# Seven block products for half the k-tiles of the output groups, on a TensorE-bound decoder trunk

## The chip, the cores and the metric

The kernel runs on one core of a Trainium2 chip. Its time is the device time of one execution in microseconds (us), less being better. Five engines work side by side, each with its own in-order queue: TensorE (PE, with PEld for the loads of its stationary operand), VectorE (DVE), ScalarE (ACT), GpSimd (POOL) and SyncE (SP). SP and POOL issue the DMAs spoken of here. They meet through semaphores alone.

## The reference

A decoder trunk of two layers, one of gated linear attention (GLA, 4 heads) and one of retention (8 heads), on 256 tokens of width 2048, all in float32. Cut to what matters:

```python
h = x
h = h + gla_mixer(rms_norm(h, gla_norm[0]), gla_w_in[0], ...)        # ends with (o * silu(gate)) @ w_out
h = h + retention_mixer(rms_norm(h, ret_norm[0]), ..., ret_w_in[0])  # ends with (o * silu(gate)) @ w_out
return rms_norm(h, final_norm)
```

`w_in` has 10240 columns (GLA) and 12288 (retention), `w_out` is 4096 x 2048 in both. Nearly all of the work is the product of 256 tokens with these weights, each read once from HBM.

## The kernel before, in words

The weights are laid out as 60 groups of 2048 rows and 512 columns. A group is 16 k-tiles of 128 rows, read in four chunks of 1 MB (`raw`, four k-tiles) by SP. For precision every chunk is split in two, `hi` (rounded to TensorE's fp32r format, ScalarE, line 152) and `lo` (the rest, VectorE, line 153), two k-tiles at a time: such a piece, 128 x 1024, is called a unit here. The pools hold three raw chunks, three `hi` and three `lo` tiles; a tile is written again only when its last reader is done, and `emit_split` runs two units ahead of the matmuls.

The tokens are split in the same way and kept on chip, as `xhl` (layer input) and `ogt` (mixer output, transposed, 16 k-tiles for one half of the inner width). A product of a k-tile with a group takes three matmuls per token half of 128 tokens: hi x hi, hi x lo, lo x hi (`mm3`, lines 189 to 191). `group_x` does this for the 16 k-tiles and both token halves, into two PSUM banks: 96 matmuls of 512 columns.

Heads come first (`gla_head`, `ret_head`): one group for q and k, then groups for v and the gate, with the scores' work of small tiles fitted in by a queue of generators (`side`; `advance` takes one step after each unit, `drain_side` takes all). After half of the heads of a layer `out_half` multiplies `ogt` with the four groups of that half of `w_out`, and `out_cols` (line 678) adds each result to `resid` on VectorE. That happens four times, under the names ga, gb (GLA) and ra, rb (retention), 16 groups in all. In gb the sums are also transposed back into `xhl` (`transpose_out`) for the next layer; in rb the last group is done by `out_tail`, which also norms and stores.

The order on each engine is set by a scheduler from the program's dependences; queues are in order when the kernel runs. POOL issues the few small loads (`dm`, `gg`, `gb`, `pos`, `fn`) and does some additions of the GLA scores.

Of the kernel before, what the change touches and what calls it, by code (L numbers as in the profile page):

```python
# [10 lines left out]
F32 = mybir.dt.float32  # L11
F32R = mybir.dt.float32r
BF16 = mybir.dt.bfloat16
I32 = mybir.dt.int32
AF = mybir.ActivationFunctionType
ALU = mybir.AluOpType

P = 128
SEQ = 256
# [3 lines left out]
GW = 512  # L23
SUB = 2
NSUB = NKT // SUB
CHUNK = 4
# [29 lines left out]
def kernel(  # L56
# [17 lines left out]
    nc = tc.nc  # L74
    pool = lambda name, bufs, **kw: ctx.enter_context(tc.tile_pool(name=name, bufs=bufs, **kw))
    one = pool("one", 1)
    raw_p = pool("raw", 3)
    hi_p = pool("hi", 3)
    lo_p = pool("lo", 3)
    v_p = pool("v", 2)  # L80
# [20 lines left out]
    per_raw = CHUNK // SUB  # L101
    raws_per_group = NKT // CHUNK

    last0 = (n_groups - 1) * NSUB

    def emit_raw(parts=1):
        c = emitted["raw"]
        if c >= n_groups * raws_per_group:
            return
        t = raw_p.tile([P, CHUNK, GW], F32, tag="raw", name=f"raw{c}")  # L110
        g, j = divmod(c, raws_per_group)
        src = w_all[g, :, j * CHUNK * GW : (j + 1) * CHUNK * GW].rearrange("p (k n) -> p k n", n=GW)
        step = CHUNK // parts
        raws[c] = t
        emitted["raw"] += 1

        def load(k, n=1):
            sl = slice(k * step, (k + n) * step)
            nc.sync.dma_start(t[:, sl, :], src[:, sl, :])

        if parts > 1:
            return load
        load(0)
# [15 lines left out]

    def emit_split(pieces=1, between=None):  # L140
        i = emitted["sub"]
        if i >= n_groups * NSUB:
            return
        c, j = divmod(i, per_raw)
        while emitted["raw"] <= min(c + DMA_LOOK, n_groups * raws_per_group - 1):
            emit_raw()
        src = raws[c][:, j * SUB : (j + 1) * SUB, :]
        hi, lo = split_tiles(i)
        step = SUB // pieces
        for k in range(pieces):  # L150
            sl = slice(k * step, (k + 1) * step)
            a = nc.scalar.activation(hi[:, sl], src[:, sl], AF.Copy)  # L152
            b = nc.vector.tensor_tensor(lo[:, sl], src[:, sl], hi[:, sl].bitcast(F32), ALU.subtract)  # L153
            if i == 0:
                first(a, b)
                if k == 0:
                    between()
        splits[i] = (hi, lo)
        if j == per_raw - 1:
            del raws[c]  # L160
        emitted["sub"] += 1

# [3 lines left out]
    def advance(n=1):  # L166
        for _ in range(n):
            while side:
                try:
                    next(side[0])  # L170
                    break
                except StopIteration:
                    side.popleft()

    def drain_side():
        while side:
            advance()

    def next_weights():
        i = state["sub"]  # L180
        while emitted["sub"] <= min(i + LOOK, n_groups * NSUB - 1):
            emit_split()
        state["sub"] += 1
        return splits.pop(i)
# [8 lines left out]
    def group_x(lhs, name, hook=None, deadline=None, bank=None):  # L193
        bank = bank or (acc_p, "acc")
        ps = [bank[0].tile([P, GW], F32, tag=bank[1], name=f"{name}_ps{t}") for t in range(2)]
        for j in range(NSUB):
            if j == deadline:
                drain_side()
            hi, lo = next_weights()
            for q in range(SUB):  # L200
                for t in range(2):
                    mm3(ps[t], lhs, j * SUB + q, t, hi, lo, q)
            if hook is not None:
                hook(j)
            advance()
        return ps

    def group_w(rhs, name, extra=None):
        ps = [acc_p.tile([P, 2, SEQ], F32, tag="acc", name=f"{name}_ps{c}") for c in range(4)]
# [383 lines left out]
    def gla_head(h):  # L593
        hw = {}
        if h > 1:
            side.appendleft(gla_decay(h, hw))
        ps = group_w(xhl, f"gqk{h}", first_group if h == 0 else None)
        drain_side()

        def scores():  # L600
            yield from gla_scores(h, hw)

        qk = t4_p.tile([P, 4, SEQ], F32, tag="qk", name=f"qk{h}", bufs=1)
        evac_w(ps, qk, f"gqk{h}")
        hw["qk"] = qk
        if h == 0:
            side.append(gate_low_rank())
        if h < 2:
            side.append(gla_decay(h, hw))
        if h > 0:  # L610
            side.append(scores())
        r, r2 = rr[:, 0, :], rr[:, 1, :]
        os_, sgs, vs = [], [], []
        sso = st_p.tile([P, 2, 2], F32, tag="sso", name=f"sso{h}")

        def o_part(gi):
            g = 2 * h + gi
            if gi == 0:
                drain_side()
            po = o_mms(hw["sc"], vs[gi], f"go{g}")  # L620
            o = o_p.tile([P, 2, GW], F32, tag="o", name=f"go{g}")
            for t in range(2):
                nc.scalar.activation(o[:, t, :], po[t], AF.Copy, scale=r[:, t : t + 1])
                nc.scalar.activation(po[t], o[:, t, :], AF.Square, accum_out=sso[:, t, gi : gi + 1])
            os_.append(o)
            if gi == 1:
                side.append(og_part(0))

        def og_part(gj):
            g = 2 * h + gj  # L630
            if gj == 0:
                yield
                m = st_p.tile([P, 2], F32, tag="m", name=f"hm{h}")
                hr = st_p.tile([P, 2], F32, tag="hr", name=f"hr{h}")
                nc.vector.tensor_tensor(m, sso[:, :, 0], sso[:, :, 1], ALU.add)
                nc.vector.tensor_scalar(m, m, 1.0 / 1024.0, EPS, ALU.mult, ALU.add)
                rsqrt(hr, m, 2, f"hr{h}")
                hw["hr"] = hr
                yield
            o, sg, hr = os_[gj], sgs[gj], hw["hr"]  # L640
            for t in range(2):
                nc.vector.scalar_tensor_tensor(
                    o[:, t, :], o[:, t, :], hr[:, t : t + 1], sg[:, t, :], ALU.mult, ALU.mult
                )
            yield
            yield from transpose_out(
                lambda t, j: o[:, t, j * P : (j + 1) * P],
                (g % 4) * 4,
                S_HG + 4 * g,
                ogt,  # L650
                f"got{g}",
            )

        for gi in range(2):
            g = 2 * h + gi

            def v_hook(j):
                if h > 0 and gi == 1 and j == 1:
                    o_part(0)

            def g_hook(j):
                if h == 0 and gi == 1 and j == 5:
                    o_part(0)
                if gi == 1 and j == (6 if h == 0 else 2):
                    o_part(1)

            if h == 0 and gi == 1:
                drain_side()
                side.append(scores())
            pv = group_x(xhl, f"gv{g}", v_hook)  # L670
            vs.append(v_evac(pv, r2, f"gv{g}"))
            sgs.append(g_evac(group_x(xhl, f"gg{g}", g_hook), r, f"gsg{g}"))
        drain_side()
        side.append(og_part(1))

    def out_cols(c, ps, t, first, final):
        dst = resid[:, t, c * GW : (c + 1) * GW]
        nc.vector.tensor_tensor(dst, ps, dst, ALU.add)
        if not first:
            square_sum(t, c)  # L680
        if final:
            nc.vector.tensor_tensor(dst, dst, fns[c], ALU.mult)

    fns = {}

    def out_half(first, final, name):
        for c in range(4):
            if final:
                fns[c] = gn_p.tile([P, GW], F32, tag="gn", name=f"fn{c}")
                nc.gpsimd.dma_start(fns[c], final_norm[c * GW : (c + 1) * GW].partition_broadcast(P))  # L690
                if c == 3:
                    break
            ps = group_x(ogt, f"{name}{c}", deadline=5)
            for t in range(2):
                out_cols(c, ps[t], t, first, final)
            if first or final:
                continue
            for _ in transpose_out(
                lambda t, j: resid[:, t, c * GW + j * P : c * GW + (j + 1) * P],
                4 * c,  # L700
                S_RN + 4 * c,
                xhl,
                f"xt2_{c}",
            ):
                pass

    def rsqrt_col(y, m, name):
        s = st_p.tile([P, 4], F32, tag="nw", name=f"{name}_nw")
# [128 lines left out]
    def ret_head(h):  # L837
# [17 lines left out]
        def o_part(j):  # L855
# [19 lines left out]
            for t in range(2):  # L875
                nc.vector.scalar_tensor_tensor(
                    o[:, t, :], o[:, t, :], a[:, t : t + 1], gb, ALU.mult, ALU.add
                )
            hw["o"] = o

        sg = g_evac(group_x(xhl, f"rg{h}", o_part), r, f"rsg{h}")

# [9 lines left out]

    for h in range(2):
        gla_head(h)
    side.append(rotary_tables())
    out_half(True, False, "ga")
    for h in range(2, 4):
        gla_head(h)
    out_half(False, False, "gb")
# [110 lines left out]
```

## Time and profile before

| what | value |
|---|---|
| three runs | 1417.96, 1420.44, 1420.67 us, median 1420.44 |
| profiled execution, first to last instruction | 1418.0 us |
| PE, DVE, ACT, POOL busy | 99%, 64%, 49%, 3% |
| loads by SP: 1 MB chunks, issue to landing | 238, median 4.8 us |
| the four output stages in the trace | 255 to 344, 582 to 673, 953 to 1041, 1320 to 1410 us |

In the rows below, a group of instructions is told as: line, engine, operation, output <- inputs, shapes, count | busy us, mean ns of one | idle us of the engine just before them and what ended most of it. PEclk gives the granted TensorE clock in tenths in 40 slices of the span. A row by stretches starts with the stretch, its length, then busy us (and instructions) of PE, PEld, DVE, ACT, POOL, the clock, the DMA engines' busy share and GB/s. In a DMA row stand queue, count, KB each and median us from issue to landing. A timeline row begins with start and length in us.

### The profile page before, as it was taken

The page shows a single profiled execution, that of the slowest core. Times are in us where ns is not written, and L with a number is a line of the kernel's source. Part 1 is how long each engine was busy: PE and PEld are TensorE (multiplying, and loading weights), DVE is VectorE, ACT ScalarE, POOL GpSimd, SP SyncE. Part 2 cuts the span into 40 slices and gives each one's busy share as a digit, 9 for nine tenths or more (in the row PEclk, how much of TensorE's full clock was granted, in tenths as well). Part 3 has the DMA queues.
Part 4 walks back from the last instruction along what each step waited for, and adds up shares of the span by engine and source line. Part 5 has one row for each costly group of instructions (what it writes and reads, how often), then busy time and mean ns, then how long its engine had stood idle before and what let it go on. Part 6 is the DMA issues. An engine that isn't in the chain of part 4 may idle for free.

```text
span 1418.0 us, 17505 instructions
## 1 busy us (share of the span) xinstructions
PE 1403.7 (99%) x6800; PEld 1181.0 (83%) x6800; DVE 907.0 (64%) x1423; ACT 693.1 (49%) x896; POOL 46.5 (3%) x99
## 2 busy tenths in 40 slices
PE   8999999999999999999999999999999999999997
PEld 6888888888888888888888888888888888888887
DVE  6685796645855774655666666665547666666664
ACT  4575655534554645554544444444344444444453
POOL 1001020000010020000000000000000000000000
PEclk9999999999999999999999999999999999999999
DMA  8654555555555555455555555555555555555562
GB/s 286 238 179 148 186 183 178 178 194 188 181 178 178 173 199 183 169 187 179 184 196 191 194 193 195 185 198 179 200 186 184 196 183 198 183 204 175 209 215 90
DMA packets 40147, 266.72 MB, mean 188 GB/s; under 512 B 4848, under 2 KB 5360, under 8 KB 9344
## 3 DMA queue, kind: packets, MB, share of 16 engines
q1 hardware_dynamic: 36816, 257.05, 52.1%
q0 software_dynamic: 2240, 7.21, 1.6%
q10 hardware_dynamic: 1008, 1.35, 0.3%
q8 instruction: 53, 0.87, 0.2%
q14 instruction: 30, 0.25, 0.0%
HBM read 263.49 MB, written 2.10 MB: 187 GB/s over the span
## 4 chain that ended last, share of the span: by engine, by line
PE 98%; DVE 0%; ACT 0%; DMA 0%; issue 0%; ACTq 0%
PE rqk_ps L232 8%; PE gv_ps L189 4%; PE gg_ps L189 4%; PE rv_ps L189 4%; PE gv_ps L190 4%; PE rv_ps L190 4%; PE gg_ps L190 4%; PE gv_ps L191 4%; PE gg_ps L191 4%; PE rv_ps L191 4%; PE rg_ps L189 4%; PE rg_ps L190 4%; PE rg_ps L191 4%; PE rqk_ps L233 4%; PE gqk_ps L232 4%; PE gb_ps L189 2%
## 5 line engine op out<-in xcount | busy, mean ns | idle before, releaser
L153 DVE TENSOR_TENSOR lo<-raw,hi 128x1024 fp32r<-128x1024 f32 (+1 forms) x473 | 576.6, 1222 | 425.0 <-ACT hi L152 424.4
L152 ACT ACTIVATE hi<-raw 128x1024 fp32r<-128x1024 f32 (+1 forms) x473 | 499.5, 1057 | 608.3 <-PE rg_ps L191 104.6
L232 PE MATMUL rqk_ps<-xhl,hi 128*128 128x512 f32 x480 | 166.9, 398 | 0.0
L233 PE MATMUL rqk_ps<-xhl,lo 128*128 128x256 f32 x480 | 126.4, 280 | 0.0
L232 PEld LDWEIGHTS rqk_ps<-xhl,hi 128*128 128x128 f32 x480 | 88.8, 188 | 17.5
L190 PE MATMUL rv_ps<-lo,xhl 128*128 128x512 f32 x256 | 100.4, 392 | 0.0
L190 PE MATMUL gv_ps<-lo,xhl 128*128 128x512 f32 x256 | 100.4, 392 | 0.0
L190 PE MATMUL gg_ps<-lo,xhl 128*128 128x512 f32 x256 | 100.4, 392 | 0.0
L191 PE MATMUL gv_ps<-hi,xhl 128*128 128x512 f32 x256 | 100.2, 392 | 0.0
L191 PE MATMUL gg_ps<-hi,xhl 128*128 128x512 f32 x256 | 100.0, 391 | 0.0
L191 PE MATMUL rv_ps<-hi,xhl 128*128 128x512 f32 x256 | 99.7, 389 | 0.0
L190 PE MATMUL rg_ps<-lo,xhl 128*128 128x512 f32 x256 | 99.6, 389 | 0.0
L191 PE MATMUL rg_ps<-hi,xhl 128*128 128x512 f32 x256 | 99.6, 389 | 0.0
L189 PE MATMUL gv_ps<-hi,xhl 128*128 128x512 f32 x256 | 93.2, 391 | 0.0
L189 PE MATMUL rv_ps<-hi,xhl 128*128 128x512 f32 x256 | 92.1, 390 | 0.0
L233 PEld LDWEIGHTS rqk_ps<-xhl,lo 128*128 128x128 f32 x480 | 89.1, 189 | 3.4
L189 PE MATMUL rg_ps<-hi,xhl 128*128 128x512 f32 x256 | 91.8, 389 | 0.0
L189 PE MATMUL gg_ps<-hi,xhl 128*128 128x512 f32 x256 | 91.7, 391 | 0.0
L232 PE MATMUL gqk_ps<-xhl,hi 128*128 128x512 f32 x216 | 73.3, 397 | 0.0
L191 PEld LDWEIGHTS rv_ps<-hi,xhl 128*128 128x128 f32 x256 | 48.1, 188 | 10.0
L191 PEld LDWEIGHTS rg_ps<-hi,xhl 128*128 128x128 f32 x256 | 48.1, 188 | 10.0
L190 PEld LDWEIGHTS rg_ps<-lo,xhl 128*128 128x128 f32 x256 | 48.1, 188 | 10.0
(273 smaller groups left out, 2405.3 us busy)
## 6 DMA issues: line engine op xcount, KB each, us to landing
raw<-in_w_all SPq DMA_DIRECT2D x238, 1024.0 KB, 4.8
resid<-in_x_n SPq DMA_DIRECT2D x2, 1024.0 KB, 8.5
gg<-in_gn_g POOLq DMA_DIRECT2D x8, 256.0 KB, 3.8
gb<-in_gn_b POOLq DMA_DIRECT2D x8, 256.0 KB, 4.5
raw<-in_w_all SPq DMA_DIRECT2D x3, 512.0 KB, 6.4
xt<-in_x_t SPq DMA_DIRECT2D x3, 512.0 KB, 8.0
dm<-in_dmat POOLq DMA_DIRECT2D x8, 192.0 KB, 2.6
fn<-in_final_norm POOLq DMA_DIRECT2D x4, 256.0 KB, 4.2
```

What stands on the lines that cost most here:

```text
L152: a = nc.scalar.activation(hi[:, sl], src[:, sl], AF.Copy)
L153: b = nc.vector.tensor_tensor(lo[:, sl], src[:, sl], hi[:, sl].bitcast(F32), ALU.subtract)
L189: mm(ps, xh, hi[:, q, :], start=kt == 0, stop=False)
L190: mm(ps, xh, lo[:, q, :], start=False, stop=False)
L191: mm(ps, xl, hi[:, q, :], start=False, stop=kt == NKT - 1)
L232: mm(ps[c], wh, rhs[:, kt, :, :], start=kt == 0, stop=False)
L233: mm(ps[c][:, 0, :], wl, rhs[:, kt, 0, :], start=False, stop=False)
```

## The change

Output groups are taken in pairs p and q (same rows of `w_out`, two neighbouring column groups), except the last two of rb, which stay as they were: seven pairs. For k-tiles 0 to 7 the 2 x 2 blocks (two token halves, two halves of those k-tiles, two column groups) are multiplied by a scheme of seven block products in place of eight; k-tiles 8 to 15 are multiplied as before (`both`). The new function `pair_x` does a pair:

- A block product (`seven`) is four k-tiles with one set of 128 tokens: 12 matmuls, from two units.
- Its token operands are plain halves or four sums of halves, which `token_combos` makes once per output half on VectorE and ScalarE, in the `side` queue of the last head.
- Its weight operands are chunk sums that are made in the raw tile: after x (first p chunk) is split, a DMA from POOL with `accum_op=ALU.add` adds another chunk to it in place, then again, three times in all; y (second q chunk) gets one. So x is split four times, y twice, and a pair has 22 units where two groups had 16. `plan_pair` writes the order.
- One PSUM bank, `a`, carries three products after each other without being cleared: after the first, second and third product `join` adds it to or subtracts it from `resid` on VectorE; it then takes k-tiles 8 to 15 of its own block. A second bank `b` is joined twice.
- The raw pool has four tiles instead of three (x stays for a whole pair), and the space for POOL's DMA descriptors is halved to 8192.

```diff
-    raw_p = pool("raw", 3)
+    raw_p = pool("raw", 4)
...
+    def plan_pair(gp, gq):
+        x = plan_chunk(gp, 0)
+        plan_units(x, False, [(x, gq, 0)])
+        plan_units(plan_chunk(gp, 1))
+        v0 = plan_chunk(gp, 2)
+        plan_units(v0)
+        y = plan_chunk(gq, 1)
+        plan_units(x, False, [(x, gq, 1)])
+        plan_units(y, False, [(y, gq, 0)])
+        v1 = plan_chunk(gp, 3)
+        units.append((v1, 0, False, ()))
+        plan_units(x, False, [(x, gp, 1)])
+        units.append((v1, 1, True, ()))
+        plan_units(y)
+        plan_units(x)
+        for j in (2, 3):
+            plan_units(plan_chunk(gq, j))
...
         splits[i] = (hi, lo)
-        if j == per_raw - 1:
+        for x, g, k in then:
+            nc.gpsimd.dma_start(raws[x], chunk_src(g, k), accum_op=ALU.add)
+        if last:
             del raws[c]
...
+        seven(a, plain(0, 0), True, True)
+        join(0, 0, a, ALU.add)
+        seven(c11, plain(1, 0), True, False)
+        c21 = acc_p.tile([P, GW], F32, tag="acc", name=f"{name}_ps21")
+        both((c11, c21), 0, (False, True), (False, False))
+        both((c11, c21), 1, (False, False), (False, False))
+        while cname not in combos:
+            advance()
+        b = lev_p.tile([P, GW], F32, tag="lev", name=f"{name}_psb")
+        seven(b, mixed(0), True, True)
+        join(0, 1, b, ALU.subtract)
+        join(1, 1, b, ALU.add)
+        c12 = acc_p.tile([P, GW], F32, tag="acc", name=f"{name}_ps12")
+        seven(c12, mixed(2), True, False)
+        drain_side()
+        both((c11, c21), 2, (False, False), (False, False))
+        seven(a, mixed(1), False, True)
+        join(0, 1, a, ALU.subtract)
+        both((c11, c21), 3, (False, False), (True, False))
+        seven(a, mixed(3), False, True)
+        join(1, 0, a, ALU.subtract)
+        done(0, 0, c11)
+        seven(c21, plain(1, 1), False, True)
+        done(1, 0, c21)
+        for j in range(4):
+            both((c12, a), j, (False, False), (j == 3, j == 3))
+        done(0, 1, c12)
+        done(1, 1, a)
...
+            def join(t, n, ps, op):
+                c = 2 * pair + n
+                dst = resid[:, t, c * GW : (c + 1) * GW]
+                with tc.high_priority():
+                    nc.vector.tensor_tensor(dst, dst, ps, op)
...
-    nc = bacc.Bacc("TRN2", target_bir_lowering=False, num_devices=1)
+    nc = bacc.Bacc("TRN2", target_bir_lowering=False, num_devices=1, dynamic_dma_scratch_size=8192)
```

The token sums, in the same diff:

```diff
+    def token_combos(lhs, name):
+        full = []
+        for half in range(2):
+            f = t4_p.tile([P, CHUNK, SEQ], F32, tag="t4", name=f"{name}_f{half}")
+            src = lhs[:, half * CHUNK : (half + 1) * CHUNK]
+            nc.vector.tensor_tensor(f, src[:, :, 0].bitcast(F32), src[:, :, 1].bitcast(F32), ALU.add)
...
+                nc.vector.tensor_tensor(u, a21, a22, ALU.subtract)
+                nc.vector.scalar_tensor_tensor(s, u, -1.0, a11, ALU.mult, ALU.subtract)
...
+                nc.vector.tensor_tensor(c[:, 0], a12, s, ALU.add)
+                nc.vector.tensor_tensor(c[:, 1], a11, a21, ALU.add)
...
+            nc.scalar.activation(d[:, 0], c, AF.Copy)
+            nc.vector.tensor_tensor(d[:, 1], c, d[:, 0].bitcast(F32), ALU.subtract)
```

More of the change, by code (lines that the diff above doesn't have):

```diff
@@ L102, with plan_chunk, plan_units, plan_group @@
     raws_per_group = NKT // CHUNK
-    last0 = (n_groups - 1) * NSUB
+    chunks, units = [], []
+    def plan_chunk(g, j):
+        chunks.append((g, j))
+        return len(chunks) - 1
+    def plan_units(c, last=True, then=()):
+        for half in range(per_raw):
+            end = half == per_raw - 1
+            units.append((c, half, last and end, then if end else ()))
+    def plan_group(g):
+        for j in range(raws_per_group):
+            plan_units(plan_chunk(g, j))
+    def plan_pair(gp, gq):
[15 more added lines that the diff above has]
+            plan_units(plan_chunk(gq, j))
+    def plan_all():
+        g = 0
+        for stage, heads in (("gla", 2), ("gla", 2), ("ret", 4), ("ret", 4)):
+            for _ in range(heads * (5 if stage == "gla" else 3)):
+                plan_group(g)
+                g += 1
+            plan_pair(g, g + 1)
+            if g + 4 == n_groups:
+                plan_group(g + 2)
+                plan_group(g + 3)
+            else:
+                plan_pair(g + 2, g + 3)
+            g += 4
+    plan_all()
+    last0 = len(units) - NSUB
+    def chunk_src(g, j):
+        return w_all[g, :, j * CHUNK * GW : (j + 1) * CHUNK * GW].rearrange("p (k n) -> p k n", n=GW)
     def emit_raw(parts=1):
         c = emitted["raw"]
-        if c >= n_groups * raws_per_group:
+        if c >= len(chunks):
             return
         t = raw_p.tile([P, CHUNK, GW], F32, tag="raw", name=f"raw{c}")
-        g, j = divmod(c, raws_per_group)
-        src = w_all[g, :, j * CHUNK * GW : (j + 1) * CHUNK * GW].rearrange("p (k n) -> p k n", n=GW)
+        src = chunk_src(*chunks[c])
         step = CHUNK // parts
@@ L141, in emit_split @@
         i = emitted["sub"]
-        if i >= n_groups * NSUB:
+        if i >= len(units):
             return
-        c, j = divmod(i, per_raw)
-        while emitted["raw"] <= min(c + DMA_LOOK, n_groups * raws_per_group - 1):
+        c, j, last, then = units[i]
+        while emitted["raw"] <= min(c + DMA_LOOK, len(chunks) - 1):
             emit_raw()
@@ L180, in next_weights @@
         i = state["sub"]
-        while emitted["sub"] <= min(i + LOOK, n_groups * NSUB - 1):
+        while emitted["sub"] <= min(i + LOOK, len(units) - 1):
             emit_split()
@@ L206, in group_x, with product @@
         return ps
+    def product(ps, a, hi, lo, q, start, stop):
+        xh, xl = a
+        mm(ps, xh, hi[:, q, :], start=start, stop=False, skip_group_check=True)
+        mm(ps, xh, lo[:, q, :], start=False, stop=False, skip_group_check=True)
+        mm(ps, xl, hi[:, q, :], start=False, stop=stop, skip_group_check=True)
+    def token_combos(lhs, name):
[4 more added lines that the diff above has]
+            nc.vector.tensor_tensor(f, src[:, :, 0].bitcast(F32), src[:, :, 1].bitcast(F32), ALU.add)
+            full.append(f)
+            yield
+        a11, a21 = full[0][:, :, 0:P], full[0][:, :, P:SEQ]
+        a12, a22 = full[1][:, :, 0:P], full[1][:, :, P:SEQ]
+        got = []
+        u, s = None, None
+        for half in range(2):
+            c = t4_p.tile([P, 2, CHUNK, P], F32, tag="t4", name=f"{name}_c{half}")
+            if half == 0:
+                u, s = c[:, 0], c[:, 1]
+                nc.vector.tensor_tensor(u, a21, a22, ALU.subtract)
+                nc.vector.scalar_tensor_tensor(s, u, -1.0, a11, ALU.mult, ALU.subtract)
+            else:
+                nc.vector.tensor_tensor(c[:, 0], a12, s, ALU.add)
+                nc.vector.tensor_tensor(c[:, 1], a11, a21, ALU.add)
+            yield
+            d = v_p.tile([P, 2, 2, CHUNK, P], F32R, tag="v", name=f"{name}_d{half}")
+            nc.scalar.activation(d[:, 0], c, AF.Copy)
+            nc.vector.tensor_tensor(d[:, 1], c, d[:, 0].bitcast(F32), ALU.subtract)
+            got.append(d)
+            yield
+        combos[name] = tuple((got[i][:, 0, k], got[i][:, 1, k]) for i, k in ((0, 0), (0, 1), (1, 0), (1, 1)))
@@ new lines, with pair_x, seven, plain @@
+    combos = {}
+    def pair_x(lhs, name, cname, join, done):
+        a = lev_p.tile([P, GW], F32, tag="lev", name=f"{name}_psa")
+        c11 = acc_p.tile([P, GW], F32, tag="acc", name=f"{name}_ps11")
+        def seven(ps, get, start, stop):
+            for half in range(2):
+                hi, lo = next_weights()
+                for q in range(SUB):
+                    k = half * SUB + q
+                    product(ps, get(k), hi, lo, q, start and k == 0, stop and k == CHUNK - 1)
+            advance()
+        def plain(part, t):
+            return lambda k: tuple(lhs[:, part * CHUNK + k, i, t * P : (t + 1) * P] for i in range(2))
+        def mixed(n):
+            return lambda k: tuple(x[:, k] for x in combos[cname][n])
+        def both(ps, j, start, stop):
+            hi, lo = next_weights()
+            for q in range(SUB):
+                for t in range(2):
+                    kt = 2 * CHUNK + j * SUB + q
+                    x = tuple(lhs[:, kt, i, t * P : (t + 1) * P] for i in range(2))
+                    product(ps[t], x, hi, lo, q, start[t] and q == 0, stop[t] and q == SUB - 1)
+            advance()
+        seven(a, plain(0, 0), True, True)
[5 more added lines that the diff above has]
+        while cname not in combos:
+            advance()
+        b = lev_p.tile([P, GW], F32, tag="lev", name=f"{name}_psb")
[18 more added lines that the diff above has]
+        done(1, 1, a)
@@ L627, in o_part @@
                 side.append(og_part(0))
+                if h % 2:
+                    side.append(token_combos(ogt, "gb" if h == 3 else "ga"))
         def og_part(gj):
@@ L684, with out_half, finish @@
     fns = {}
[L686 to L697, printed above, removed]
+    def out_half(first, final, name, later=None):
+        def finish(t, c, ps):
+            out_cols(c, ps, t, first, final)
+            if first or final or t == 0:
+                return
             for _ in transpose_out(
@@ L705, in out_half, with load_fn @@
                 pass
+        for pair in range(1 if final else 2):
+            if pair == 1 and later is not None:
+                side.append(later)
+            for c in (2 * pair, 2 * pair + 1) if final else ():
+                load_fn(c)
+            def join(t, n, ps, op):
[3 more added lines that the diff above has]
+                    nc.vector.tensor_tensor(dst, dst, ps, op)
+            pair_x(ogt, f"{name}{pair}", name, join, lambda t, n, ps: finish(t, 2 * pair + n, ps))
+        if final:
+            load_fn(2)
+            load_fn(3)
+            ps = group_x(ogt, f"{name}2", deadline=5)
+            for t in range(2):
+                out_cols(2, ps[t], t, first, final)
+    def load_fn(c):
+        fns[c] = gn_p.tile([P, GW], F32, tag="gn", name=f"fn{c}")
+        nc.gpsimd.dma_start(fns[c], final_norm[c * GW : (c + 1) * GW].partition_broadcast(P))
     def rsqrt_col(y, m, name):
@@ L879, in o_part @@
             hw["o"] = o
+            if h % 4 == 3:
+                side.append(token_combos(ogt, "rb" if h == 7 else "ra"))
         sg = g_evac(group_x(xhl, f"rg{h}", o_part), r, f"rsg{h}")
@@ L894 @@
         gla_head(h)
-    side.append(rotary_tables())
-    out_half(True, False, "ga")
+    out_half(True, False, "ga", rotary_tables())
     for h in range(2, 4):
```

## The prediction

> **What bounds the kernel now.** I read the page's busy shares and its chain first, then the largest groups.
>
> ```profile
> PE 1403.7 (99%) x6800; PEld 1181.0 (83%) x6800; DVE 907.0 (64%) x1423; ACT 693.1 (49%) x896; POOL 46.5 (3%) x99
> ...
> PEclk9999999999999999999999999999999999999999
> DMA  8654555555555555455555555555555555555562
> ...
> PE 98%; DVE 0%; ACT 0%; DMA 0%; issue 0%; ACTq 0%
> ...
> L153 DVE TENSOR_TENSOR lo<-raw,hi 128x1024 fp32r<-128x1024 f32 (+1 forms) x473 | 576.6, 1222 | 425.0 <-ACT hi L152 424.4
> L152 ACT ACTIVATE hi<-raw 128x1024 fp32r<-128x1024 f32 (+1 forms) x473 | 499.5, 1057 | 608.3 <-PE rg_ps L191 104.6 <-PE rqk_ps L232 78.0 <-PE gg_ps L191 72.9
> ```
>
> TensorE is the chain (98%), at full clock. The two split engines wait on each other and on TensorE; the DMA engines are a little over half used. So fewer matmuls is a real gain, as long as hi and lo still arrive in time. How much room they have shows in the timeline of one plain output group.
>
> ```profile
> 967.69 0.62 PE L189 MATMUL ra_ps<-hi,ogt 128*128 128x512 f32 x2
> ...
> 967.95 1.06 ACT L152 ACTIVATE hi<-raw 128x1024 fp32r<-128x1024 f32 x1 [1.67 <-PE ra_ps L191]
> ...
> 969.04 1.23 DVE L153 TENSOR_TENSOR lo<-raw,hi 128x1024 fp32r<-128x1024 f32 x1 [1.50 <-ACT hi L152]
> ...
> 970.41 0.62 PE L189 MATMUL ra_ps<-hi,ogt 128*128 128x512 f32 x2
> 970.61 1.06 ACT L152 ACTIVATE hi<-raw 128x1024 fp32r<-128x1024 f32 x1 [1.60 <-PE ra_ps L191]
> ...
> 973.13 0.62 PE L189 MATMUL ra_ps<-hi,ogt 128*128 128x512 f32 x2
> ```
>
> A unit (two k-tiles, 12 matmuls) takes 970.41 to 973.13, 2.72 us, so one matmul has 0.2267 us (the 389 ns of the groups overlap). A split starts 0.2 us after TensorE leaves the unit three back (970.41 to 970.61: the buffers are three deep), takes 1.06 + 1.23 us and leaves VectorE idle 1.5 us per unit.
>
> **The matmuls.** In a block product (a unit of the new `seven`) a unit feeds one token half only, as the order on TensorE shows at the second ga pair. Before:
>
> ```order
> L189 MATMUL ga1_ps0_2424<-hi89_2406,ogt_101 128x512
> L190 MATMUL ga1_ps0_2424<-lo89_2407,ogt_101 128x512
> L191 MATMUL ga1_ps0_2424<-hi89_2406,ogt_101 128x512
> L189 MATMUL ga1_ps1_2425<-hi89_2406,ogt_101 128x512
> L190 MATMUL ga1_ps1_2425<-lo89_2407,ogt_101 128x512
> L191 MATMUL ga1_ps1_2425<-hi89_2406,ogt_101 128x512
> ```
>
> After (psa is the chained bank):
>
> ```order
> L262 MATMUL ga1_psa_2568<-hi103_2549,ogt_101 128x512
> L263 MATMUL ga1_psa_2568<-lo103_2550,ogt_101 128x512
> L264 MATMUL ga1_psa_2568<-hi103_2549,ogt_101 128x512
> L262 MATMUL ga1_ps11_2569<-hi104_2572,ogt_101 128x512
> L263 MATMUL ga1_ps11_2569<-lo104_2573,ogt_101 128x512
> ```
>
> A k-tile's weights now serve 3 matmuls instead of 6. Per pair, 8 block products of 12 matmuls become 7: 12 fewer, in 7 pairs 84 x 0.2267 = **-19.0 us**. The price is units: 22 per pair instead of 16 (42 more splits in all), 14 of them only 6 x 0.2267 = 1.36 us long.
>
> **Joins among short units.** VectorE needs 1.23 of those 1.36 us for lo, and now also five joins per pair (0.68 us each):
>
> ```profile
> L678 DVE TENSOR_TENSOR resid<-ra_ps,resid 128x512 f32<-128x512 f32 x8 | 5.1, 682 | 0.0
> ```
>
> On VectorE in the second ga pair, before (one group's end, then the next):
>
> ```order
> L678 TENSOR_TENSOR resid_99<-ga0_ps0_2231,resid_99 128x512
> L678 TENSOR_TENSOR resid_99<-ga0_ps1_2232,resid_99 128x512
> L153 TENSOR_TENSOR lo90_2429<-raw45_2326,hi90_2428 128x1024
> L153 TENSOR_TENSOR lo91_2445<-raw45_2326,hi91_2444 128x1024
> L153 TENSOR_TENSOR lo92_2463<-raw46_2388,hi92_2462 128x1024
> ```
>
> After (raw47 is x, raw50 is y, raw51 a plain chunk; lo112 is unit 10 of the pair, counted from 0):
>
> ```order
> L203 TENSOR_TENSOR lo111_2681<-raw50_2570,hi111_2680 128x1024
> L859 TENSOR_TENSOR resid_99<-resid_99,ga1_psb_2667 128x512 x2
> L203 TENSOR_TENSOR lo112_2701<-raw51_2598,hi112_2700 128x1024
> L203 TENSOR_TENSOR lo113_2711<-raw47_2474,hi113_2710 128x1024
> L203 TENSOR_TENSOR lo114_2732<-raw47_2474,hi114_2731 128x1024
> L203 TENSOR_TENSOR lo115_2749<-raw51_2598,hi115_2748 128x1024
> L203 TENSOR_TENSOR lo116_2759<-raw50_2570,hi116_2758 128x1024
> L859 TENSOR_TENSOR resid_99<-resid_99,ga1_psa_2568 128x512
> ```
>
> Two joins stand ahead of lo112, with three short units behind it. In a run of short units lo arrives 0.4 us ahead of need (two units, 2.72, plus the 0.23 of the first hi matmul, less 0.2 + 1.06 + 1.23 + 0.06); two joins are 1.36, VectorE's own gaps hold 0.3, so unit 10 is late by 0.7, the unit behind the first join by 0.1 to 0.2. I take 0.8 per pair, **+6 us**; ends 0 and all joins, 5 x 0.68 x 7 = 24. The chained bank itself is cheap: a join is done within about 2 us of its product, and a 2.72 us unit lies between the products of the chain.
>
> **The adding DMAs.** On POOL, before, at head 1's scores and after them head 2's:
>
> ```order
> L586 TENSOR_TENSOR s32_1_1535<-s32_1_1535,m1_1788 128x2x32 x2
> L586 TENSOR_TENSOR s32_1_1535<-s32_1_1535,m1_1788 128x64 x2
> L586 TENSOR_TENSOR s32_2_3067<-s32_2_3067,m2_3320 128x64 x2
> L586 TENSOR_TENSOR s32_2_3067<-s32_2_3067,m2_3320 128x32x2 x2
> L586 TENSOR_TENSOR s32_2_3067<-s32_2_3067,m2_3320 128x16x4 x2
> ```
>
> After:
>
> ```order
> L928 DMA pos_2593<-in_positions 128x256
> L210 DMA raw40_2074<-in_w_all 128x2048 x2
> L210 DMA raw43_2250<-in_w_all 128x2048
> L210 DMA raw40_2074<-in_w_all 128x2048
> L210 DMA raw47_2474<-in_w_all 128x2048 x2
> L210 DMA raw50_2570<-in_w_all 128x2048
> ```
>
> Four 1 MB adds per pair, 28 in all, stand between the two heads' work, each held until the splits of its chunk are read; behind them on POOL only work of the next head waits (in the last pair a row of final_norm). ScalarE, in order, waits for each add, and all later splits with it. With TensorE's unit 0 at time 0, the units give each add a budget:
>
> - x, first add: split of unit 1 ends at -0.2; unit 6 is due at 4 x 1.36 + 2 x 2.72 = 10.9, its split 2.2 earlier (1.06 + 1.23 + hand-over - 0.23). Budget 8.9 us.
> - x, second: the split of unit 7 starts when unit 4 is done (8.4), ends at 10.9 with the handovers; unit 11 is due at 10.9 + 4 x 1.36 + 2.72 + 0.8 = 19.9. Budget 19.9 - 2.2 - 10.9 = 6.8, say 6.7 with semaphores.
> - y: split of unit 9 ends at 14.9, unit 14 is due at 25.3: 8.2.
> - x, third: split of unit 12 ends at 20.1, unit 16 is due at 28.0: 5.7; and 4.7 once the second add has been the wait.
>
> So with L us from issue to landing a pair loses nothing up to L = 5.7, then L - 5.7, and above 6.7 (L - 6.7) + (L - 4.7) = 2L - 11.4.
>
> What is L? The trace has no add. Nearest:
>
> ```profile
> raw<-in_w_all SPq DMA_DIRECT2D x238, 1024.0 KB, 4.8
> gg<-in_gn_g POOLq DMA_DIRECT2D x8, 256.0 KB, 3.8
> gb<-in_gn_b POOLq DMA_DIRECT2D x8, 256.0 KB, 4.5
> dm<-in_dmat POOLq DMA_DIRECT2D x8, 192.0 KB, 2.6
> ...
> GB/s 415 360 0 0 0 186 295 404 426 87 11 0 164 197 426 404 229 0 0 153 131 382 470 262 0 0 44 164 328 437 382 44 0 0 186 251 426 426 109 0
> ```
>
> The same bytes by SP's queue land in 4.8 (low end, if reading the target costs nothing and POOL's queue starts as soon). The last row (1000 to 1030 us, slices of 0.75) shows 426 GB/s while a load streams: 1.05 MB in 2.46 us. If source and target are read one after the other, L is 4.8 + 2.46 = 7.3; and POOL's 256 KB take 3.8 to 4.5, up to 1.8 more than their bytes' share of 4.8 explains (4.8 - 0.75 x 2.46 = 3.0): high end 9.1. I take 7.0, near the doubled read, with some overlap of the two: 2.6 per pair, **+18 us**; ends 0 and 6.8 x 7 = 48.
>
> The Trainium skill ("Collectives: The Full Stack", section on the bandwidth ceiling) holds that an adding DMA is slow not for the add but for its two source reads through one ring, about half a copy's rate. By it L would be 7.3 and the sum some 4 us higher; no run here shows it yet.
>
> DMA load: 7 loads and 4 adds per pair, 11 to 15 MB of reads where 8 were, at 0.55 share now: 0.76 to 1.0. That alone is no bound, at the upper end nearly one.
>
> **Other work that loses its cover.**
>
> ```profile
> L258 DVE SCALAR_TENSOR_TENSOR ogt<-got_tp,smalls,ogt 128x256 fp32r<-128x256 f32 x32 | 14.3, 477 | 0.9 <-ACT ogt L257 0.6
> L642 DVE SCALAR_TENSOR_TENSOR go<-go,hr,gsg 128x512 f32<-128x512 f32 x16 | 11.5, 747 | 0.4
> L808 DVE TENSOR_TENSOR ra<-rqk,trig 128x1024 f32<-128x1024 f32 x8 | 9.8, 1224 | 0.3
> L811 DVE TENSOR_TENSOR rb<-rqk,trig 128x512 f32<-128x512 f32 x8 | 5.5, 685 | 0.0
> ...
> 230.00:255.00 25.00, 25.00 (x116) 20.80 (x115) 15.75 (x28) 13.53 (x20) 0.00 (x0) 1.00 0.49 168
> ...
> 931.00:953.00 22.00, 22.00 (x99) 18.22 (x98) 16.10 (x31) 7.95 (x9) 1.07 (x2) 1.00 0.57 208
> ...
> L488 ACT ACT_TABLE_LOAD x4 | 5.1, 1283 | 0.1
> L487 ACT ACTIVATE ya<-y,smalls 128x256 f32<-128x256 f32 x8 | 3.8, 478 | 0.0
> ```
>
> The last head's output still passes through VectorE in the first pair of ga and gb: between the lo of units 1 and 2, 4 x 0.477 + 2 x 0.747 = 3.4 us where 1.5 are free, so 2 late each; the transposes of the next layer's input in gb's second pair I put at 2. ScalarE's decay work of head 2 (4 x 0.478 + 1.28 = 3.2 us) stands ahead of a short-unit stretch's hi in ga's first pair, where x's second add is awaited anyway: 0, or 2 if that add is early. **+6** (ends 0 and 14). The token sums cost VectorE 4 x 1.22 + 4 x 0.69 = 7.7 us per half, four times, in the last gate group. In the GLA window it has 25 - 15.75 = 9.3 idle (fits), in the retention window 22 - 16.1 = 5.9: 1.8 over, twice, **+3**. ScalarE's 2.1 fit in both windows.
>
> **Sum.** -19.0 + 6 + 18 + 6 + 3 = +14. The profiled execution is itself 1418.0 us, 2.4 under the median of 1420.44; on the median: **1434 us**, slower by 1.0%.
>
> **Rivals.**
> - *The add costs a load* (L to 5.7). The GB/s row speaks for it: the engines idle half the time. The adds vanish: -4, 1416 us; if the side work hides too, 1406. It decides from L = 5.9 down. Chance 0.33 of a gain beyond 0.2%.
> - *It cancels* (L about 6.2: 0.5 x 7 = 4, against the -4 above): 1418 to 1423, chance 0.12. A difference of 0.2% (2.8 us) is what a measurement of this kernel can tell.
> - *The queue or the add is slower still* (L over 9.1, loads of SP interleaved with it): from 1463 up, chance 0.11. Here single waits pass 3 us. The Trainium skill ("TensorE: Matmul & The Clock Gate") says that the clock halves after about 3.4 us of idleness. PEclk is 9 in every slice here, so no run yet shows it; a digit under 9 in the out stages would.
>
> The forecast itself has 0.44. Slower in all: 0.44 + 0.11 = 0.55. The range 1406 to 1463 leaves out most of the third rival and about 0.08 of the first.
>
> **What would show it.** 84 fewer matmuls at 0.227; "ACT hi <- DMA raw" rising from nothing to some 18 us or more, at the third and fourth use of x; landing of raw<-in_w_all on POOL's queue near 7 us; VectorE's lo after the psb joins late by under 1 us. A landing near 5, or waits on DMA near zero, makes the forecast wrong; if it is slower with adds near 5, the splits are the cause.

## The result and the profile after

The changed kernel takes 1457.7 us (median of 1451.4 to 1462.8) against 1420.2 us: ratio 1.027, 95% interval 1.0254 to 1.0286. It is slower by 37.5 us where I had forecast 14. The profiled execution has a span of 1456.1 us, 38.1 more than before. Busy times, clock and DMA share in slices, the chain, the two split groups, and the loads on the two queues, from the page:

```profile
PE 1404.6 (96%) x6716; PEld 1172.4 (81%) x6716; DVE 997.2 (68%) x1532; ACT 740.8 (51%) x946; POOL 75.1 (5%) x127
...
PEclk9999999999999999999999999999999999999999
DMA  8554555968554555789565555569865555555881
...
PE 24%; DMA 3%; issue 1%; DVE 1%; ACT 1%; ACTq 0%; POOLq 0%
...
L203 DVE TENSOR_TENSOR lo<-raw,hi 128x1024 fp32r<-128x1024 f32 (+1 forms) x515 | 623.9, 1220 | 368.3 <-ACT hi L202 367.1
L202 ACT ACTIVATE hi<-raw 128x1024 fp32r<-128x1024 f32 (+1 forms) x515 | 541.0, 1057 | 602.7 <-PE rg_ps L243 97.9
...
raw<-in_w_all SPq DMA_DIRECT2D x231, 1024.0 KB, 4.8
raw<-in_w_all POOLq DMA_DIRECT2D x28, 1024.0 KB, 8.2
```

The 84 matmuls are gone (6800 to 6716), and yet TensorE's busy share fell from 99 to 96% of a longer span. DMA now stands in the chain (which could be followed back no further than to 1025 us, so its shares add up to some 30%). An add lands 8.2 us after its issue, where I took 7.0. PEclk hides something: a 9 stands for 90% or more, so a stretch of 3.4 us at half clock (below) doesn't show in a slice of 36 us, and the digit under 9 that I had named as a sign did not appear. The waits of ScalarE name the place, and the waits of the adds say how long they take at best and at worst:

```profile
ACT hi L202 <- DMA raw<-in_w_all: 69.2, 21, 7.5
```

```profile
who waited for it (us, times):
  ACT hi L202: 68.8, 20
...
DMA to landing us min/median/max: 7.9/8.2/12.4
```

Before, no split in the out stages waited for a DMA, but for four of the last weights in rb (4.0 us in all). Now 68.8 us of ScalarE's waiting, 20 waits in seven pairs, end with an adding DMA. One pair (the first of ra) in order of time; the four POOL rows are its adds, x, x, y, x:

```profile
975.96 0.89 POOL L210 DMA_DIRECT2D raw<-in_w_all  x1 [5.13 <-DVE lo L203]
...
984.74 1.06 ACT L202 ACTIVATE hi<-raw 128x1024 fp32r<-128x1024 f32 x1 [2.16 <-DMA raw<-in_w_all]
...
988.83 0.86 POOL L210 DMA_DIRECT2D raw<-in_w_all  x1 [11.97 <-DVE lo L203]
...
992.43 0.86 POOL L210 DMA_DIRECT2D raw<-in_w_all  x1 [2.74 <-DVE lo L203]
...
996.94 2.00 ACT L202 ACTIVATE hi<-raw 128x1024 fp32r<-128x1024 f32 x2 [4.70 <-DMA raw<-in_w_all]
...
998.03 2.36 DVE L203 TENSOR_TENSOR lo<-raw,hi 128x1024 fp32r<-128x1024 f32 x2 [3.56 <-ACT hi L202]
...
998.05 0.50 PE L262 MATMUL ra_psa<-hi,ra_d 128*128 128x512 f32 x1 [3.72 <-ACT hi L202]
...
1000.37 0.63 PE L264 MATMUL ra_ps<-hi,ogt 128*128 128x512 f32 x1
...
1000.69 0.85 POOL L210 DMA_DIRECT2D raw<-in_w_all  x1 [7.39 <-DVE lo L203]
...
1008.96 2.96 ACT L202 ACTIVATE hi<-raw 128x1024 fp32r<-128x1024 f32 x3 [2.89 <-DMA raw<-in_w_all]
...
1011.33 0.50 PE L263 MATMUL ra_ps<-lo,ogt 128*128 128x512 f32 x1 [0.70 <-DVE lo L203]
```

Read the x rows as one chain. The add of 975.96 lands, hi runs at 984.74; the second add is issued at 988.83, when the second lo is done; it lands, hi runs at 996.94, TensorE goes on at 998.05 after 3.7 us; the third add is issued at 1000.69, 3.75 us after that hi began, and hi waits again until 1008.96. The interval is 12.87 us from the first add to the second and 11.86 from the second to the third (12.1 to 13.0 and 11.8 to 12.7 in the seven pairs). The chain that the profile follows back from the last instruction is the same one, here in the second pair of ra (start, length, what):

```profile
1037.82 8.20 DMA raw<-in_w_all
...
1046.13 1.06 ACT hi L202
...
1047.21 2.37 DVE lo L203 x2
...
1049.87 8.25 DMA raw<-in_w_all
...
1058.22 1.07 ACT hi L202
...
1059.32 1.24 DVE lo L203
...
1060.60 0.50 PE ra_ps L263
```

From 1037.82 to 1060.60 TensorE doesn't stand in it. Two more things stand in the rows of the first pair. The matmul of 1000.37 has 0.63 us where 0.39 is usual: TensorE ran at half clock. And only one matmul of x's unit starts at 998.05, then matmuls on `ogt` follow: these belong to the unit before. The order on TensorE shows why (the same place in the first pair of gb; hi215 is x's, hi214 that of the plain unit before):

```
2690 L262 MATMUL gb0_psa_4875<-hi215_5015,gb_d0_4866 128x512 [waits Activation_49]
2691 L263 MATMUL gb0_ps11_4876<-lo214_5006,ogt_101 128x512 [waits DVE_49]
2692 L264 MATMUL gb0_ps11_4876<-hi214_5005,ogt_101 128x512
...
2700 L264 MATMUL gb0_ps21_4933<-hi214_5005,ogt_101 128x512
2701 L263 MATMUL gb0_psa_4875<-lo215_5016,gb_d0_4866 128x512 [waits DVE_49]
```

The scheduler put the first matmul that waits for the sum ahead of ten that could have run (2.27 us of cover).

### The profile page after: what moved, and what is told of

Same layout as the page of the kernel before. It is cut to its first block, busy times and chain, and to the rows that moved or that the text cites. A ratio compares the mean times of both kernels' runs of the same rounds, so it can differ in the third digit from the quotient of the medians.

```text
span 1456.1 us, 17623 instructions
## 1 busy us (share of the span) xinstructions
PE 1404.6 (96%) x6716; PEld 1172.4 (81%) x6716; DVE 997.2 (68%) x1532; ACT 740.8 (51%) x946; POOL 75.1 (5%) x127
## 3 DMA queue, kind: packets, MB, share of 16 engines
q0 software_dynamic: 6272, 36.57, 12.7%
## 5 line engine op out<-in xcount | busy, mean ns | idle before, releaser
L203 DVE TENSOR_TENSOR lo<-raw,hi 128x1024 fp32r<-128x1024 f32 (+1 forms) x515 | 623.9, 1220 | 368.3 <-ACT hi L202 367.1
L202 ACT ACTIVATE hi<-raw 128x1024 fp32r<-128x1024 f32 (+1 forms) x515 | 541.0, 1057 | 602.7 <-PE rg_ps L243 97.9
L241 PEld LDWEIGHTS rg_ps<-hi,xhl 128*128 128x128 f32 x256 | 48.1, 188 | 10.0
L243 PEld LDWEIGHTS rg_ps<-hi,xhl 128*128 128x128 f32 x256 | 48.0, 188 | 10.0
```

Of the source, the lines that this page charges most:

```text
L241: mm(ps, xh, hi[:, q, :], start=kt == 0, stop=False)
L243: mm(ps, xl, hi[:, q, :], start=False, stop=kt == NKT - 1)
```

## The experiments

The theories: the adds against the splits and joins (A, B); the second read against POOL's queue (A1, A2); and, for how an add costs time, the matmul at the head of the queue (H), the half clock (K), the load on the DMA engines (D), or x's own chain of adds and splits, whatever TensorE does in between (C). Ratios are against the kernel before, on the same chip.

**No adds.**

```diff
-        for x, g, k in then:
-            nc.gpsimd.dma_start(raws[x], chunk_src(g, k), accum_op=ALU.add)
```

> The changed kernel without its 28 adding DMAs: x and y are split again and again as first loaded, so the weight sums are left out of the products; everything else (84 fewer matmuls, 42 more splits, joins, token sums) stays. Theory A (the adds are the whole loss): the stalls that end with a landing go, and with them the stretches at half clock; 1420.2 - 19.0 + some 4 us of late lo in the first pair of ga = 1405, range 1400 to 1411. Theory B (the short units, the joins and the side work cost about what I put them at, 15 us, or more): 1416 or above.

1403.3 us, ratio 0.9896 (0.9881 to 0.9911). Its page:

```profile
PE 1386.1 (99%) x6716; PEld 1163.4 (83%) x6716; DVE 997.1 (71%) x1532; ACT 744.0 (53%) x946; POOL 50.7 (4%) x99
```

B falls. Without the adds the products lack the weight sums, and all else is the same. The adds are worth 1457.7 - 1403.3 = 54 us, more than the whole loss. All else that I had added up to 15 us (joins, side work, token sums) is 1403.3 - (1418.0 - 19.0) = 4.3 us, with 1418.0 the kernel before on that chip.

**Copies in place of adds.**

```diff
-            nc.gpsimd.dma_start(raws[x], chunk_src(g, k), accum_op=ALU.add)
+            nc.gpsimd.dma_start(raws[x], chunk_src(g, k))
```

> The same 28 DMAs on POOL's queue, at the same places and of the same size, but plain copies in place of adds (so x and y hold the last block read, not sums). Theory A1 (the second read of the adding DMA is what makes it slow): packets of 0.31 us in place of 0.63, landing 1.6 + 8 x 0.31 + 0.5 = 4.6 us after issue, under the 5.7 us of the tightest budget; 1405 to 1412, like the kernel without adds. Theory A2 (POOL's queue is slow whatever it carries): landing near 8 us and 1450 or more.

1406.4 us, ratio 0.9915 (0.9901 to 0.993). The copies land in 5.0 us:

```profile
raw<-in_w_all POOLq DMA_DIRECT2D x28, 1024.0 KB, 5.0
```

Same queue, same places, same size: A2 falls, and what costs is the add, not the queue. Whether its time goes into the second read (A1) or into the addition itself, these runs don't tell apart. In the traces an 8 KB packet took 0.629 us in an add, 0.309 in a copy (medians). The share of POOL's queue in the DMA engines' span says it too; first before, then after, then with copies:

```profile
q0 software_dynamic: 2240, 7.21, 1.6%
```

```profile
q0 software_dynamic: 6272, 36.57, 12.7%
```

```profile
q0 software_dynamic: 6272, 36.57, 7.8%
```

Less the 1.6% of the other loads, 28 adds take 11.1% of 1456 us, 5.8 us of every engine each; 28 copies take 6.2% of 1405 us, 3.1 us.

**The order on TensorE.** In block products, and in `both`, lo comes first, so that no matmul of the next unit is ready early:

```diff
-        mm(ps, xh, hi[:, q, :], start=start, stop=False, skip_group_check=True)
-        mm(ps, xh, lo[:, q, :], start=False, stop=False, skip_group_check=True)
+        mm(ps, xh, lo[:, q, :], start=start, stop=False, skip_group_check=True)
+        mm(ps, xh, hi[:, q, :], start=False, stop=False, skip_group_check=True)
```

> The changed kernel with the lo product first in each block product and in the second half of the k-tiles, which puts TensorE's queue into the order of the program: the ten matmuls of the unit before x's second sum no longer stand behind the first matmul that waits for that sum. Theory H (that matmul at the head of the queue is the loss): 10 x 0.227 us of cover in each of 7 pairs come back, and the stalls fall under the length that halved the clock: 1430 to 1442. Theory C (a pair lasts as long as x's own chain of three adds and the splits between them, wherever TensorE waits): the stall at the second sum shrinks by about 2.3 us and the one at the third grows by as much; 1450 to 1460.

1476.8 us, ratio 1.0419 (1.0401 to 1.0436): neither. H falls, since the time rose by 19 us; C's figure is missed too, though its sign holds. The same place in the first pair of ra, at the third sum:

```profile
1014.11 2.95 ACT L202 ACTIVATE hi<-raw 128x1024 fp32r<-128x1024 f32 x3 [5.44 <-DMA raw<-in_w_all]
...
1016.48 0.50 PE L262 MATMUL ra_ps<-lo,ogt 128*128 128x512 f32 x1 [3.31 <-DVE lo L203]
```

The wait moved in part to the third sum, as C says, and grew: 0.7 us there before, 3.3 now, with 2.8 left at the second. A unit that waits now waits for lo, about 1.2 us after hi, and the third add of this pair landed after 9.5 us where it took 8.2, with 112 packets of SP's loads among its own instead of 51. Over the seven pairs the third add lands after 9.6 us in the median, 1.3 later than in the changed kernel, so the two would make 7 x (1.2 + 1.3) = 18 of the 19 us. That is an estimate; it was not tried.

**TensorE kept busy in the wait**, by 18 or 12 matmuls with zeros ahead of the product that waits for the second sum:

```diff
+        for k in range(18):
+            mm(c12, zeros, lhs[:, k % NKT].rearrange("p i t -> p (i t)"), start=False, stop=False, skip_group_check=True)
```

> The changed kernel with 18 matmuls by a tile of zeros (4.1 us, added to an open sum) ahead of the product that waits for x's second sum, in each pair: TensorE waits 4 us less and its clock should stay full there. Theory K (the half-speed stretches after the long stalls add their 12.6 us to the time): 1445 to 1449. Theory C (x's chain of adds and splits sets the end of each pair; a slow TensorE between two sums costs nothing, since the third sum is late anyway): 1454 to 1462, with the stall before the second sum gone and longer waits at the third.

1465.6 us, ratio 1.0332 (1.0315 to 1.035); 18 were too many to tell: they take 4.1 us, and no such wait of the changed kernel was over 3.9. With 12:

> The changed kernel with 12 zero matmuls (2.7 us) in each pair's wait for x's second sum, less than the 3.5 to 4.1 us that six of the seven pairs wait there. Theory K (the half-speed stretches add to the time): no half clock at that place, 1445 to 1449. Theory C (the sums set the end of the pair, and a slow TensorE in between costs nothing): 1454 to 1462, the waits at the third sum longer by what the clock no longer takes.

1461.3 us, ratio 1.030 (1.0287 to 1.0314). The mean clock rose from 0.987 to 0.994 (the row has span and clock):

```profile
core 0: 1459.9 us, clock 0.994
```

So half of the time at half clock is gone, and 7 x 2.7 = 19 us of work more is done, for about 4 us. K falls: the slow stretches lay in the shadow of the next add. From TensorE's side the loss of the changed kernel looks like some 37 us of waits in the four output stages and 31 us at half clock, but keeping the clock up doesn't give the second part back. C stands, and the chain itself shows it. In the three runs that changed what TensorE does (lo first, 18 and 12 zero matmuls) x's second add follows the first after 12.4, 12.5 and 12.5 us, as in the changed kernel (12.4), and the third follows the second after 11.9, 11.9 and 12.5 (11.9 there; medians over the pairs). From the second landing to the third issue it is 3.85 us in all four.

**Half adds, and another order.** Two adds of 512 KB in place of one, each issued when its own two k-tiles are split:

```diff
-            units.append((c, half, last and end, then if end else ()))
+            units.append((c, half, last and end, then))
...
-            nc.gpsimd.dma_start(raws[x], chunk_src(g, k), accum_op=ALU.add)
+            sl = slice(j * SUB, (j + 1) * SUB)
+            nc.gpsimd.dma_start(raws[x][:, sl], chunk_src(g, k)[:, sl], accum_op=ALU.add)
```

> The changed kernel with each adding DMA cut in two of 512 KB, each issued as soon as its own two k-tiles are split. Theory C (x's chain of splits and adds is the pair's length): in each of the three links the first half starts about 1.4 us earlier and the second half is needed 1.4 us later, 2.7 us per link against 6 us of waiting and 1.8 us of half clock per pair: most of the waits go, 1405 to 1418, on the fast side of the kernel before. If 4 KB packets take as long as 8 KB ones (0.63 us), the second halves land 5 us later than now and the time is 1470 or more. If the splits and joins were the loss, 1450.

1448.6 us, ratio 1.0206 (1.0186 to 1.0225): better by 9 us, far less than C's figure. It is near the 1450 named for the splits and joins, but the run without adds had ruled these out. The half adds don't land in half the time:

```profile
raw<-in_w_all POOLq DMA_DIRECT2D x56, 512.0 KB, 7.5
```

A half by itself landed in 5.5 us at best, but x's second add and y's meet in one queue, and the last of their four halves took 8.3 to 9.3 us, x's last half 9.5 to 12. With whole adds and a longer gap between x's uses (`pair_x` takes its products in the same new order):

```diff
-        units.append((v1, 0, False, ()))
-        plan_units(x, False, [(x, gp, 1)])
-        units.append((v1, 1, True, ()))
+        plan_units(v1)
+        plan_units(x, False, [(x, gp, 1)])
         plan_units(y)
-        plan_units(x)
-        for j in (2, 3):
-            plan_units(plan_chunk(gq, j))
+        plan_units(plan_chunk(gq, 2))
+        q3 = plan_chunk(gq, 3)
+        units.append((q3, 0, False, ()))
+        plan_units(x)
+        units.append((q3, 1, True, ()))
```

> That order with whole adds. x's budgets become 8.9, 8.7 and 10.7 us against landings of 8.0 to 8.3, so x no longer waits; y's add, issued 4 us behind x's second in the same queue, has 7.4 us and lands after about 9. Theory C with that queue: about 1.6 us of waiting per pair, at y's second use, little half clock: 1410 to 1420. If the tail of ten matmuls behind the first waiting one is what costs (theory H), 1440.

1455.9 us, ratio 1.0268 (1.0252 to 1.0285): the gain that I expected is not there. In this order the adds land later still:

```profile
DMA to landing us min/median/max: 7.9/9.0/12.1
```

Longer gaps in the order of the units made no link shorter: x's adds are issued 12.8 and 11.9 us after each other, no closer than before, and y's add and x's last land after 10.8 and 9.9 us (9.5 and 8.3 in the changed kernel; medians). I had given y about 9. In the first pair of ra the long wait now ends with y's add, issued at 986.55 and landed at 997.63:

```profile
997.74 2.95 ACT L203 ACTIVATE hi<-raw 128x1024 fp32r<-128x1024 f32 x3 [4.71 <-DMA raw<-in_w_all]
...
1000.74 0.80 PE L263 MATMUL ra_ps<-hi,ogt 128*128 128x512 f32 x1 [3.32 <-ACT hi L203]
```

With both:

> The same half adds, and the units in another order: both units of v1 ahead of x's third use, and the q chunks (but for the last unit) ahead of x's fourth, so that all three gaps between x's uses are long. Theory C: no add is waited for; as without adds, 1401 to 1408. If the packets of the adds themselves hold up loads or other work (21 to 26 MB more of DMA traffic per stage), it stays above 1412.

1430.6 us, ratio 1.0073 (1.0054 to 1.0092): about half of TensorE's waits are gone (some 18 us of 37 are left), and the DMA engines are nearly full. In the second pair of ra (columns as in the rows by stretches before):

```profile
1002.00:1044.00 42.00, 37.25 (x153) 29.57 (x152) 27.54 (x28) 19.06 (x19) 6.90 (x8) 0.92 0.95 259
```

DMA share 0.95. A pair needs 4 adds x 8 packets x 0.629 + 7 loads x 8 x 0.309 = 37.4 us on every DMA engine (38.3 with the half adds, whose 4 KB packets took 0.328 us), and its TensorE work is 180 matmuls, 40.8 us. In this order adds and loads hold each other up: a load of SP, 4.8 us elsewhere, took up to 9.9 us there, and a half add landed 12.4 us after its issue.

**Which add.** Seven of 28 left out, x's second or y's:

```diff
-        plan_units(x, False, [(x, gq, 1)])
+        plan_units(x, False)
```

> The changed kernel without x's second add (7 of 28; the third and fourth use of x then take the sum of two blocks instead of three and four). Theory C (the chain of x's splits and adds): a whole link goes, the longest waits with it; x's third add has 5.7 us and lands after 8.1, so about 2.4 us and 0.8 for lo are left per pair: 1424 to 1436. Theory D (the adds cost by their load on the DMA engines, whichever they are): a quarter of the adds gives back a quarter of the 54 us, 1440 to 1446.

1442.2 us, ratio 1.0166 (1.0148 to 1.0185).

```diff
-        plan_units(y, False, [(y, gq, 0)])
+        plan_units(y, False)
```

> The changed kernel without y's add (also 7 of 28, the same megabytes; y's second use takes the block as loaded). Theory C: y is not in x's chain and its landing is covered today, so nearly nothing: 1450 to 1457. Theory D: a quarter again, 1440 to 1446.

1452.7 us, ratio 1.023 (1.0215 to 1.0246). The same bytes are worth some 15 us in x's chain and 5 outside it, so D alone doesn't hold. But C's figure for the first is missed by 6 us or more, and the trace of that run says why (first pair of ra; POOL's rows are y's add and x's last):

```profile
979.59 0.87 POOL L210 DMA_DIRECT2D raw<-in_w_all  x1 [15.41 <-DVE lo L203]
984.18 0.86 POOL L210 DMA_DIRECT2D raw<-in_w_all  x1 [3.73 <-DVE lo L203]
...
987.77 2.01 ACT L202 ACTIVATE hi<-raw 128x1024 fp32r<-128x1024 f32 x2 [2.40 <-DMA raw<-in_w_all]
...
994.18 2.96 ACT L202 ACTIVATE hi<-raw 128x1024 fp32r<-128x1024 f32 x3 [4.41 <-DMA raw<-in_w_all]
```

x's last add, issued 4.6 us behind y's, lands 9.9 us later. When y's add landed, 131 of the queue's 8 KB packets had ended since its issue, and one add is 128: the queue carries one add after the other. So it is C with that queue in it.

**In gb alone**, half adds and the other order in two pairs, all other groups as before (`if name != "gb"`: `group_x` and `out_cols` as in the kernel before).

> The half adds in the other order of units, in the two pairs of gb alone; ga, ra and rb as in the kernel before. In the run with all seven pairs gb's two waited 1.0 and 1.9 us, against 2.7 us of saved matmuls each: 5.4 - 2.9 = 2.5 us under the kernel before, less the token sums: 1415 to 1417, at the edge of what can be told from no change. If the DMA engines, nearly full in a pair, are the bound there too: 1418 or above.

1417.7 us against 1419.4, ratio 0.9986 (0.9977 to 0.9995). Of the versions that compute the whole product it is the one below both kernels, by no more than can just be told. In the two stretches below, one for each pair, TensorE is idle for 0.97 and 1.53 us, near what was expected, although the DMA share is 0.96 and 0.99: nearly full DMA engines alone don't cost what the pairs of ra lost.

```profile
575.00:615.00 40.00, 39.03 (x179) 31.35 (x178) 30.67 (x35) 23.62 (x31) 6.91 (x8) 1.00 0.96 244
619.00:657.00 38.00, 36.47 (x166) 29.45 (x165) 30.68 (x36) 25.83 (x36) 6.89 (x8) 1.00 0.99 255
```

## Why the prediction was right or wrong

The direction and the cause were right: stalls at the third and fourth use of x, with the adds behind them. The size was not, and neither was the share of the two places. By the steps:

- **Matmuls, -19.0.** Right: 84 fewer, and without the adds the time is 4.3 us above 1418.0 - 19.0.
- **Joins +6, side work +6, token sums +3.** Too high: 4.3 us for all three. In the run without adds 1.2 of them are two waits in ga's first pair (0.64 and 0.52 us), behind ScalarE's decay work and table load, which I had put at "0, or 2". Of the late lo behind the joins no wait of over 0.3 us is left there.
- **Adding DMAs, +18: the step that failed.** The runs show 54. The 54 is measured; its parts are an account after the fact, read from the trace, and no run changes one of them alone. First, L: 8.2 us, not 7.0. I took the doubled read with some overlap; the packets leave room for none, with 0.629 us for an add against 0.309 for a copy. The page "Collectives: The Full Stack" of the Trainium skill, section on the bandwidth ceiling, says of ReduceScatter that it is slow not for its add but for the two source reads, and runs at half a copy's rate. The trace agrees on the rate. The doubled read was 7.3; most of the rest is POOL's later first packet, 1.6 us after issue, where a load of SP alone has 0.96. Each pair pays L twice: 2 x 1.2 x 7 = 17 us. Second, the hand-overs: by my budgets the second add of x is issued 11.1 us after the first, and the third 2.4 + L after the second, 10.6. The trace has 12.4 and 11.9 as medians. From a sum's landing to the next add go two hi, two lo and a semaphore, 3.85 us (1046.02 to 1049.87 in the chain above), where I had counted one split: 2 x 1.3 x 7 = 18 us. 18 + 17 + 18 = 53.
- **The sum.** 14 + 17 + 18 - 11 = 38; measured 37.5. No part of it needs the half clock. That the time lies inside the range is in part luck: with L at 8.2 the forecast's own terms give 1434 + 17 = 1451, and the room above that was meant for an L of up to 9.1, not for the hand-overs.
- **Slips in the working.** The high end of L takes POOL's small loads as up to 1.8 us late, but 4.5 - 3.0 is 1.5, so it should have been 8.8. The bounds 1406 and 1463 come out as 1407 and 1464 from the terms given. Nothing above hangs on them.
- **What I did not see.** The ten matmuls behind the waiting one stood in the order, and I did not price them. My budgets with L = 7.0 put 0.3 us of a pair's wait at the second sum and 2.3 at the third; the first pair of ra has 3.7 and 0.7. By the reading as a chain, the ten move the wait from the third sum to the second and cost little; the run that put lo first made units wait for lo as well, so no run shows their price alone.
- **DMA load, "0.76 to 1.0, nearly a bound".** 0.91 in the pair above (973 to 1013 us). That it becomes the bound once the chain is shortened isn't shown: ra's pairs lost time at 0.95, gb's lost little at 0.96 and 0.99.
- **The third rival, the clock gate.** Half clock did come, though the chain hid it, and not by the length of one wait. In the changed kernel (stretch, length, PE, PEld, DVE, ACT, POOL busy, clock, DMA share, GB/s):

```profile
613.36:616.78 3.42, 2.11 (x10) 1.41 (x8) 2.24 (x3) 0.01 (x1) 0.86 (x1) 1.00 0.99 206
616.78:620.19 3.41, 1.43 (x6) 1.19 (x7) 1.45 (x2) 2.01 (x2) 0.00 (x0) 1.00 1.08 214
620.19:623.60 3.41, 3.41 (x10) 2.63 (x9) 0.92 (x1) 0.89 (x1) 0.85 (x1) 0.50 0.81 127
...
326.64:330.05 3.41, 1.59 (x8) 0.97 (x6) 1.73 (x2) 0.00 (x0) 0.56 (x1) 1.00 1.10 219
330.05:333.47 3.42, 1.93 (x8) 1.61 (x9) 1.95 (x2) 2.01 (x2) 0.00 (x0) 1.00 0.94 194
```

Both waits were 3.30 us long. One fell so that TensorE was busy for 1.43 us of a stretch of 3.41, and the next stretch ran at 0.50. The other left 1.59 and 1.93 busy, and the clock stayed. The page "TensorE: Matmul & The Clock Gate" of the Trainium skill, part on the HAM clock gate, says that the clock halves after an idle window of some 3.4 us, and that this window runs free of the kernel. The trace agrees on the window's length, but the window needn't be idle all through: here 1.98 us of one was enough, and what counted was the idle time within the window.

## What to carry to other kernels

Where a tile is used, changed in place by a DMA and used again, price it as a chain (landing, every split that has to read it, the issue, the landing) and compare the chain's length with the work between the uses; idle engines and a half-free DMA don't shorten it. An accumulating DMA cost twice the engine time of a copy here: 4 of them took as much as 8 loads, for 12 matmuls (2.7 us) saved. Once a chain sets the end, a faster clock or extra work in its shadow moves the wait and little of the time (19 us of zero products cost 4).

## What the runs showed of the hardware

- An adding DMA of 1 MB into SBUF takes 0.629 us per 8 KB packet against 0.309 for a copy, starts 1.6 us after its issue on POOL when it is alone in its queue, and lands after 7.9 us at the least. The queue carries one add after the other: y's, issued some 4 us behind x's, landed after 9.0 to 11.2 us.
- Half clock comes in stretches of 3.41 us on a fixed grid: in the changed kernel slow ones start at 285.68 and 620.19 us, 98 such stretches apart. In the nine runs with adds in all seven pairs, between 240 us and the last 30 us, each of the 44 stretches in which TensorE, after full clock, idled for 1.9 us or more was followed by a slow one, and none with under 1.75; between them both occur. One wait of 1.92 us inside a stretch (282.27 to 285.68) was enough.
